# A layer of hybrid attention: transposed probabilities read back in one DMA instead of four

## The chip, the cores and the metric

One core of a Trainium2 chip runs the whole kernel. The metric is the device time of one execution in microseconds. The engines are named as in the profile: PE (TensorE; its weight loads are PEld), DVE (VectorE), ACT (ScalarE), POOL (GpSimd) and SP (SyncE, which here only issues DMAs).

## The reference, cut to what matters

One layer (DEPTH 1) works on x of 512 tokens by 1024 features, in float32:

```
h = rmsnorm(x); proj = h @ w_in              # columns go to groups A, B, C
A: 6 heads, dilated sliding-window attention, three (window, dilation) branches mixed by their denominators
B: 4 heads, gated linear attention in chunks
C: 6 heads, block attention: own block (causal) and the past blocks
x = x + concat(A, B, C) @ w_out
x = x + relu(rmsnorm(x) @ w_ff1)^2 @ w_ff2
return rmsnorm(x)
```

With 512 tokens the twelve heads of A and C can all be computed as causal attention over four query blocks and four key blocks of 128, with a bias table that counts how many branches see a distance. Each head needs, for every query block qb, scores against the keys up to its own block, an exponential P, and the product of P with the values. P comes out with queries on partitions; the product with the values needs keys on partitions. So P has to be transposed in blocks of 128 by 128.

## The kernel before, in words

Every matrix product in float32 precision is split into high and low parts and done as three faster products (names ending in h and l: wh and wl for weights, xh and xl, Ah and Al). The splitting keeps ACT and DVE busy all the time: ACT rounds (wh), DVE subtracts (wl).

The order of work comes from a planner written into the kernel. Generators ("streams") yield one operation at a time; the class Plan keeps a clock for each engine, gives each operation a cost (class Op), and issues the operation that can start first. So the order in each engine's queue is fixed when the program is built, from these modelled costs. `Shadow(op, sent)` plans with the cost of `op` but sends the operations in `sent` instead, or nothing when that is empty.

The stages are: the first projections and the norm (to 30 us), linear attention B (to about 105 us, partly beside the next one), the softmax attention of the twelve heads (about 87 to 190 us, with the query, key and value projections `qkps` and `vps` between), the output projection, and the feed-forward part in four steps to the end.

Heads are handled in pairs: p = 0 to 5, and e = 0, 1 within a pair. For each head, function `attention` computes the scores of query blocks 3, 2, 1, 0 on PE into two PSUM banks (tile `sps`, tag "s"), the widest first, 512, 384, 256 and 128 keys. Function `softmax` adds the bias and takes the row minimum on DVE in one instruction (the profile calls it CUSTOM_DVE_ANT_0, P<-sps,nb, followed by a short read of `mn`), which also frees the score bank, and then ACT forms the exponential in place.

The first five pairs (XP) are transposed by function `moved`; the last pair by PE itself. In `moved`, DVE transposes 32 by 32 blocks: for each of the four partition groups of 32 queries and each 32 keys, queries and keys change places. The results go to tile t (`tb` in the profile, blocks of query rows 3, 2 and 0) and to t2 (`t2s`, query block 1 of both heads of the pair). Since a 32 by 32 block cannot leave its group of 32 partitions, the rest of the transpose is done by way of HBM: SP stores the tile to a DRAM tensor (`turn`), and function `back` reads it to `thb` and `th` in the other order, issued by POOL. Writing a for the group of 32 queries, k for which 32 of a key block's 128 keys, j for the key among these and c for the rest, partition a*32+j of t holds columns (k, c); `back` wants partition k*32+j to hold columns (a, c). One access pattern over partitions cannot step through k and j with two different steps, so `back` issues four DMAs, one for each k, with 32 partitions each.

Function `values` then multiplies on PE (`po`), pairs (0, 1), (2, 3) and (4, 5) together, first the blocks from `thb`, then those from `th`. `mix_out` scales the result on DVE into `h`, from which the output projection follows.

SP's queue holds the stores of `turn`, the tables `nb`, the denominators (`zt`, `rzb`) and the loads of weights, in the planner's order. POOL's queue at that time holds nothing but the reads of `turn`.

Of the kernel before, what the change touches and what calls it, by code (L numbers as in the profile page):

```python
# [124 lines left out]
PE, ACT, DVE, POOL, SP = (Engine(n) for n in ("tensor", "scalar", "vector", "gpsimd", "sync"))  # L125


class Plan:
# [18 lines left out]
    def fire(self, key, t=None):  # L147
        self.done[key] = self.now if t is None else t

    def give(self, res):  # L150
        self.free[res].append(self.now)
# [79 lines left out]
def hybrid_block_kernel(ctx: ExitStack, tc: tile.TileContext, x0_d, xT_d, x_d, w0_d, wv_d, wqk_d, w1_d, w2_d,  # L231
# [13 lines left out]
    def slot(name, dt=F32, shape=(128, 512)):  # L245
        return sp.tile(list(shape), dt, name=name, tag="slot", bufs=SLOTS)

    def big(name, dt=F32, shape=(128, 1024)):
        return wp.tile(list(shape), dt, name=name, tag="big", bufs=BIGS)
# [741 lines left out]
    def attention(e):  # L991
# [7 lines left out]
        for p in range(6):  # L999
# [34 lines left out]
            if p in XP:  # L1034
                spawn(moved(p, e, P), 1)
                continue
# [86 lines left out]
    def moved(p, e, P):  # L1123

        yield ("take", "big")
        t, th = big("tb"), st["th", p, e]
        if ("t2", p) not in st:
            st["t2", p], st["th2", p] = slot("t2s"), slot("th2")
        t2, th2 = st["t2", p], st["th2", p]
        tv, t2v = (x.rearrange("p (k b j) -> p k b j", k=4, j=32) for x in (t, t2))  # L1130
        for qb, dst in ((3, tv[:, :, :4]), (2, tv[:, :, 4:7]), (1, t2v[:, :, 2 * e:2 * e + 2]), (0, tv[:, :, 7:])):
            yield ("wait", (p, e, qb))
            yield DVE.transpose(dst, P[qb].rearrange("p (b k j) -> p k b j", k=4, j=32))
        both = ("turned", p) in plan.done
        fire(("turned", p))
        d = dr.tile([128, 1024], F32, name=f"turn{2 * p + e}")
        yield SP.dma_start(d, t)
        give("big")
        if both:
            d2 = dr.tile([128, 512], F32, name=f"turn{12 + p}")  # L1140
            yield SP.dma_start(d2, t2)
            fire(("sent", p))
        yield from back(th, d)
        if both:
            yield from back(th2, d2)
            fire(("thx", p))

    def back(dst, d):
        n = d.shape[1]
        for k in range(4):  # L1150
            yield POOL.dma_start(dst[k * 32:k * 32 + 32].rearrange("p (a c) -> p a c", a=4),
                                 bass.AP(tensor=d.tensor, offset=d.offset + k * (n // 4), ap=[[n, 32], [32 * n, 4], [1, n // 4]]))

    def turned(pt, n, off, kbs, key):
        if kbs == (2,):
# [965 lines left out]
```

## Time and profile before

| | |
|---|---|
| median of 3 runs | 552.42 us (551.62 to 552.6) |
| profiled execution, its own time | 551.57 us |
| its span, first to last instruction | 549.8 us |
| busy: PE, DVE, ACT, POOL | 542.1, 486.5, 367.3, 94.6 us |
| granted TensorE clock, mean | 0.998 |
| read from HBM, written to it | 99.97 MB, 8.71 MB |

The profile is of one execution. "Busy" is time with an instruction on the engine. Each group of instructions has its outputs and inputs by name, its shape, a count, total busy microseconds and the mean nanoseconds of one, then the idle time of the engine just before and what ended it. Nearly all instructions carry line 158, the helper that sends them, so groups are told apart by tile names. In the timeline, a bracket at the end of a row gives idle time before the instruction and the instruction that ended it.

### The profile page before, as it was taken

Reading aid. Unit: us, or ns where it says so; the run is one execution under the profiler, and the core shown is the slowest. Engines: PE = TensorE matmul, PEld = TensorE weight load, DVE = VectorE, ACT = ScalarE, POOL = GpSimd, SP = SyncE. Lnnn points to the kernel's source line nnn. Section 1 sums busy time; section 2 is a strip of 40 time slices with the busy share of each in tenths; the row PEclk is TensorE's granted clock in tenths of the full one; section 3 lists DMA queues with packets and bytes.
Section 4 is the critical chain, followed back from the end, with each engine's and each line's share of the span. In section 5 each row is a group of like instructions: output and inputs, shape, how many; then the busy total and the mean of one; then the engine's idle time right before and its main releaser. Section 6 shows DMA issues by size and latency. Waiting matters only on the chain.

```text
span 549.8 us, 9220 instructions
## 1 busy us (share of the span) xinstructions
PE 542.1 (99%) x3362; PEld 474.2 (86%) x3362; DVE 486.5 (88%) x820; ACT 367.3 (67%) x628; POOL 94.6 (17%) x148
## 2 busy tenths in 40 slices
PE   9999999999999999999999999999999999999995
PEld 8988888888888788899988999888999888998884
DVE  6879998999987899899999869899679899589985
ACT  7756465668576566987965458773387863489844
POOL 7100000432624010230111100111100111202030
PEclk9999999999999999999999999999999999999999
DMA  8940304799998999889859934869744789976504
GB/s 294 395 161 2 115 1 134 223 272 256 272 310 280 345 348 241 156 227 255 234 124 287 278 60 149 229 154 268 191 110 159 161 226 246 195 167 169 103 0 153
DMA packets 35677, 109.28 MB, mean 199 GB/s; under 512 B 5266, under 2 KB 5952, under 8 KB 35632
## 3 DMA queue, kind: packets, MB, share of 16 engines
q1 hardware_dynamic: 25104, 74.81, 38.8%
q0 software_dynamic: 10240, 33.35, 31.6%
q8 instruction: 26, 0.43, 0.3%
q10 hardware_dynamic: 288, 0.53, 0.3%
q14 instruction: 19, 0.16, 0.1%
HBM read 99.97 MB, written 8.71 MB: 198 GB/s over the span
## 4 chain that ended last, share of the span: by engine, by line
PE 98%; DVE 1%; ACT 0%; issue 0%; DVEq 0%; ACTq 0%
PE f2X L158 19%; PE f1V L158 17%; PE qkps L158 12%; PE f2W L158 10%; PE vps L158 8%; PE f1W L158 8%; PE f2Y L158 5%; PE f1X L158 4%; PE sps L158 3%; PE po L158 2%; PE av L158 2%; PE lp L158 1%; PE bk L158 1%; PE bq L158 1%; PE op L158 1%; PE warm L158 1%
## 5 line engine op out<-in xcount | busy, mean ns | idle before, releaser
L158 DVE TENSOR_TENSOR wl<-w2raw,wh 128x1024 fp32r<-128x1024 f32 x56 | 67.8, 1221 | 3.3 <-ACT wh L158 3.0
L158 DVE TENSOR_TENSOR wl<-w1raw,wh 128x1024 fp32r<-128x1024 f32 x46 | 55.5, 1222 | 16.2 <-ACT wh L158 16.2
L158 PE MATMUL f1V<-Uh,wh 128*128 128x512 f32 (+1 forms) x240 | 69.1, 353 | 0.0
L158 POOL DMA_DIRECT2D w2raw<-in_w x36 | 31.6, 992 | 205.3 <-DVE wl L158 139.7
L158 ACT ACTIVATE wh<-w1raw 128x1024 fp32r<-128x1024 f32 x49 | 50.7, 1052 | 23.0 <-DVE w1raw L158 20.4
L158 ACT ACTIVATE wh<-w2raw 128x1024 fp32r<-128x1024 f32 x56 | 57.9, 1050 | 11.7 <-issue 5.1
L158 PE MATMUL f2X<-wh,Ah 128*128 128x512 f32 (+1 forms) x160 | 62.4, 390 | 0.0
L158 PE MATMUL f2X<-wh,Al 128*128 128x512 f32 (+1 forms) x160 | 61.9, 387 | 0.0
L158 PE MATMUL f2X<-wl,Ah 128*128 128x512 f32 (+1 forms) x160 | 61.9, 387 | 0.0
L158 PE MATMUL f1V<-Uh,wl 128*128 128x256 f32 x192 | 54.3, 283 | 0.0
L158 PEld LDWEIGHTS f1V<-Uh,wh 128*128 128x128 f32 x240 | 42.0, 189 | 5.8
L158 ACT ACTIVATE h<-h 128x512 f32<-128x512 f32 x56 | 35.2, 628 | 13.3 <-DVE h L158 12.6
L158 PE MATMUL qkps<-xh,wh 128*128 128x512 f32 x96 | 38.1, 397 | 0.0
L158 PE MATMUL qkps<-xh,wl 128*128 128x512 f32 x96 | 37.6, 391 | 0.0
L158 PE MATMUL qkps<-xl,wh 128*128 128x512 f32 x96 | 37.5, 391 | 0.0
L158 ACT ACTIVATE P<-P,mn 128x512 f32<-128x512 f32 (+3 forms) x48 | 26.6, 556 | 15.7 <-DVE mn L158 15.5
L158 PEld LDWEIGHTS f1V<-Uh,wl 128*128 128x128 f32 x192 | 36.4, 189 | 0.0
L158 PEld LDWEIGHTS f2X<-wh,Ah 128*128 128x128 f32 x160 | 30.1, 188 | 7.2 <-issue 1.2
L158 PEld LDWEIGHTS f2X<-wl,Ah 128*128 128x128 f32 x160 | 30.1, 188 | 6.2
L158 PEld LDWEIGHTS f2X<-wh,Al 128*128 128x128 f32 x160 | 30.1, 188 | 5.9
L158 ACT ACTIVATE Ah<-s 128x512 fp32r<-128x512 f32 x40 | 24.0, 622 | 12.8 <-DVE s L158 12.3
L158 POOL DMA_DIRECT2D thb<-turn x40 | 21.8, 552 | 59.7 <-DMA turn<-tb 41.5
(312 smaller groups left out, 1595.0 us busy)
## 6 DMA issues: line engine op xcount, KB each, us to landing
w2raw<-in_w SPq DMA_DIRECT2D x42, 512.0 KB
w2raw<-in_w POOLq DMA_DIRECT2D x36, 512.0 KB, 7.6
w1raw<-in_w SPq DMA_DIRECT2D x33, 512.0 KB
wraw<-in_wqk SPq DMA_DIRECT2D x12, 512.0 KB
turn<-tb SPq DMA_DIRECT2D x10, 512.0 KB
thb<-turn POOLq DMA_DIRECT2D x40, 128.0 KB, 5.0
w1raw<-in_w POOLq DMA_DIRECT2D x9, 512.0 KB, 6.3
wraw<-in_wv SPq DMA_DIRECT2D x8, 512.0 KB
```

The source lines that it names most:

```text
L158: getattr(getattr(self.nc, op.eng), op.method)(*op.args, **op.kw)
```

## The change

```diff
@@ moved
         for qb, dst in ((3, tv[:, :, :4]), (2, tv[:, :, 4:7]), (1, t2v[:, :, 2 * e:2 * e + 2]), (0, tv[:, :, 7:])):
             yield ("wait", (p, e, qb))
-            yield DVE.transpose(dst, P[qb].rearrange("p (b k j) -> p k b j", k=4, j=32))
+            yield DVE.transpose(dst, P[qb].rearrange("p (b j k) -> p k b j", k=4, j=32))
@@ back
         n = d.shape[1]
+        whole = POOL.dma_start(dst.rearrange("p (a c) -> p a c", a=4),
+                               bass.AP(tensor=d.tensor, offset=d.offset, ap=[[n // 4, 128], [32 * n, 4], [1, n // 4]]))
         for k in range(4):
-            yield POOL.dma_start(dst[k * 32:k * 32 + 32].rearrange("p (a c) -> p a c", a=4),
-                                 bass.AP(tensor=d.tensor, offset=d.offset + k * (n // 4), ap=[[n, 32], [32 * n, 4], [1, n // 4]]))
+            part = POOL.dma_start(dst[k * 32:k * 32 + 32].rearrange("p (a c) -> p a c", a=4),
+                                  bass.AP(tensor=d.tensor, offset=d.offset + k * (n // 4), ap=[[n, 32], [32 * n, 4], [1, n // 4]]))
+            yield Shadow(part, () if k else (whole,))
```

A key of a block was numbered k*32+j: block k held 32 neighbouring keys. Now it is j*4+k: block k holds every fourth key, starting at k. After the 32 by 32 transposes, key j*4+k stands on partition a*32+j in columns (k, c), that is, in DRAM at (a*32+j)*n + k*n/4 + c. With the partition q = j*4+k this is 32*a*n + q*n/4 + c: one step, n/4, over all 128 partitions. So one DMA reads what four did, to the same places as before, and the product with the values is unchanged.

DVE's transposes read P with the 32 elements of a block 16 bytes apart instead of 4; what they write has the same shape and place. There are 40 of them. The reads go from 60 DMAs to 15, of the same bytes and the same runs of 1 KB (512 bytes for the second tensor). The planner still sees four DMAs at their old costs, in `part`, and sends `whole` in place of the first.

## The prediction

> **What bounds the kernel now.** I read the page's head and chain first, then the list of who waited for whom on the matrix engine, then busy time by stretches.
>
> ```profile
> span 549.8 us, 9220 instructions
> PE 542.1 (99%) x3362; PEld 474.2 (86%) x3362; DVE 486.5 (88%) x820; ACT 367.3 (67%) x628; POOL 94.6 (17%) x148
> PE 98%; DVE 1%; ACT 0%; issue 0%; DVEq 0%; ACTq 0%
> PE warm L158 <- DVE eps L158: 1.1, 1, 1.1
> 268.00:540.00 272.00, 272.00 (x1546) 239.45 (x1545) 238.15 (x314) 179.00 (x270) 35.52 (x40) 1.00 0.67 169
> ```
>
> PE is the chain for 98% of the span, and the only wait of its matmuls that the list names is 1.1 us at the very start. From 268 to 540 us it is busy in all 272.00 us: a microsecond that PE loses earlier is never made up. So a gain has to come out of waits that PE hardly has, while a loss needs only an engine that falls behind PE. The change touches DVE, SP's data, POOL and the DMA queues during the attention stage, so the second view is that stage (columns: stretch, length, then busy time of PE, PEld, DVE, ACT, POOL).
>
> ```profile
> 94.68:106.00 11.32, 11.32 (x68) 9.89 (x67) 11.07 (x36) 10.08 (x27) 3.46 (x7) 1.00 0.57 189
> 106.00:122.00 16.00, 16.00 (x79) 13.52 (x79) 15.52 (x35) 8.79 (x16) 6.31 (x12) 1.00 0.95 287
> 122.00:149.00 27.00, 27.00 (x193) 23.17 (x192) 26.27 (x76) 18.41 (x47) 12.09 (x23) 1.00 0.95 262
> 149.00:164.00 15.00, 15.00 (x72) 12.48 (x71) 12.76 (x36) 11.04 (x27) 4.34 (x8) 1.00 1.03 294
> sum 69.32, PE 69.32 PEld 59.06 DVE 65.62 ACT 48.31 POOL 26.20; mean PE 17.33 PEld 14.76 DVE 16.40 ACT 12.08 POOL 6.55
> ```
>
> Here DVE is full too: 65.62 of 69.32 us, 3.70 us idle. Two engines are at their limit at once, and the coupling between them is tight:
>
> ```profile
> 94.68 1.17 DVE L158 STREAM_TRANSPOSE tb<-P 128x512 f32<-128x512 f32 x2
> 95.77 0.40 DVE L158 STREAM_TRANSPOSE t2s<-P 128x256 f32<-128x256 f32 x1
> 96.10 0.65 DVE L158 CUSTOM_DVE_ANT_0 P<-sps,nb 128x512 f32<-128x512 f32 x1
> 96.82 0.19 PEld L158 LDWEIGHTS sps<-k,q 128*128 128x128 f32 x1 [0.23 <-DVE mn L158]
> ```
>
> Transposes stand in DVE's queue directly ahead of the score minimum (P<-sps), which empties one of two score banks; PE's next score weights are loaded only when it has done so, and here PE's loader already waits 0.23 us for it. What a transpose takes longer, this wait takes longer.
>
> **The change, part by part.** (1) The transposes. Four per head, ten heads (five pairs p of two), all inside this stage:
>
> ```profile
> L158 DVE STREAM_TRANSPOSE tb<-P x30: 266/552/707, 94.7 to 162.8; 128x512 f32<-128x512 f32 x10, 128x384 f32<-128x384 f32 x10, 128x128 f32<-128x128 f32 x10
> 94.68:163.10 68.42, 14.96 (x30) 1.00 0.91 260
> 94.68:163.10 68.42, 4.05 (x10) 1.00 0.91 260
> ```
>
> They are busy for 14.96 + 4.05 = 19.01 us. Their count, sizes and destinations stay. The order in which they read P changes: the 32 elements of a block were neighbours (4 bytes apart), now each stands 16 bytes after the last. No DVE row of this trace reads in steps of 16 bytes, so the price is bounded. Nearest rows:
>
> ```profile
> 43.47 0.74 DVE L158 TENSOR_TENSOR e<-b 128x256 f32<-128x256 f32 x2
> 56.85 0.76 DVE L158 TENSOR_TENSOR e<-b 128x256 f32<-128x256 f32 x2
> L158 DVE TENSOR_TENSOR wl<-wraw,wh 128x1024 fp32r<-128x1024 f32 x8 | 9.6, 1218 | 0.0
> L158 DVE TENSOR_TENSOR la<-la,ab 128x512 f32<-128x512 f32 x1 | 0.7, 684 | 0.0
> L158 DVE TENSOR_TENSOR rg<-rg,gw 128x256 f32<-128x256 f32 x4 | 1.7, 425 | 0.1
> L158 DVE TENSOR_SCALAR sg<-rg 128x256 f32<-128x256 f32 x4 | 1.1, 286 | 0.0
> ```
>
> The seven levels of the linear attention read b in ever finer steps; the last, level 1, takes every second element (8 bytes), and its pair costs 0.76 us against 0.74 for a coarser level. So 8 bytes are as good as free; lower bound zero (a gain would need a pace that contiguous reads do not have). The pace: 1218 - 684 = 534 ns for 512 more elements, 1.04 ns each, one step per element. The fastest DVE row, sg, needs (425 - 286)/256 = 0.54 ns less per element than rg: it takes two neighbours, 8 bytes, per step. Both rows fit a reader that covers 8 bytes per step: then elements 8 bytes apart cost nothing and elements 16 bytes apart cost two steps. That is my estimate: 1.04 ns more per element. One head has 512 + 384 + 256 + 128 = 1280 elements per partition, so 1280 x 1.04 = 1.33 us more, ten heads 13.3 us. The upper end is the whole instruction doubled, fixed part too: 19.0 us. I take 13.3 because the fixed part has no reading in it.
>
> [...]
>
> How much of 13.3 us reaches PE? DVE's own pauses swallow some. Those that wait for PE in this stretch:
>
> ```profile
> 121.87 0.69 DVE L158 CUSTOM_DVE_ANT_0 P<-sps,nb 128x512 f32<-128x512 f32 x1 [0.16 <-PE sps L158]
> 124.41 0.56 DVE L158 CUSTOM_DVE_ANT_0 P<-sps,nb 128x384 f32<-128x384 f32 x1 [0.15 <-PE sps L158]
> 131.06 0.69 DVE L158 TENSOR_TENSOR tk<-qkps,R 128x512 f32<-128x512 f32 x1 [0.17 <-PE qkps L158]
> 149.35 0.69 DVE L158 TENSOR_TENSOR tk<-qkps,R 128x512 f32<-128x512 f32 x1 [0.43 <-PE qkps L158]
> 152.52 0.69 DVE L158 CUSTOM_DVE_ANT_0 P<-sps,nb 128x512 f32<-128x512 f32 x1 [1.17 <-PE sps L158]
> 156.85 0.42 DVE L158 CUSTOM_DVE_ANT_0 P<-sps,nb 128x256 f32<-128x256 f32 x1 [0.63 <-PE sps L158]
> ```
>
> They add up to 0.16 + 0.15 + 0.17 + 0.43 + 1.17 + 0.63 = 2.7 us (3.7 us with every small gap of the stretches above). I take 2.7: 13.3 - 2.7 = 10.6 us of delay for PE. DVE's longer pauses after 166 us help DVE catch up, not PE. What is queued behind a late transpose: on DVE the next minima and the splitting of weights, both awaited by PE; on SP the store of the turned tile, and behind it the loads of the next weights, which slip by as much as PE itself does.
>
> (2) The reads back. Fifteen groups of four DMAs become fifteen DMAs of the same bytes, so 45 issues on POOL go.
>
> ```profile
> L158 POOL DMA_DIRECT2D thb<-turn x40 | 21.8, 552 | 59.7 <-DMA turn<-tb 41.5 <-PE ptp L158 14.8 <-PE qkps L158 2.1
> L158 POOL DMA_DIRECT2D th<-turn x20 | 10.9, 550 | 1.3 <-issue 0.8 <-DMA thb<-turn 0.4
> L158 POOL DMA_DIRECT2D w2raw<-in_w x36 | 31.6, 992 | 205.3 <-DVE wl L158 139.7 <-DMA w2raw<-in_w 41.0 <-PE f2X L158 15.3
> 123.50 2.19 POOL L158 DMA_DIRECT2D th<-turn x4 [0.16 <-issue]
> DMA to landing us min/median/max: 5.1/7.7/8.3
> 134.94 0.61 PE L158 MATMUL po<-th,v 128*64 128x128 f32 x8
> ```
>
> POOL spends 32.7 us on sixty; fifteen at between 0.55 (today's) and 2.2 us (four times the pieces) cost 8 to 33 us, so POOL gets between 24 us and nothing back. I take 0.99, the row of a 512 KB DMA: 15 us. None of it is on the path: POOL is 17% busy and mostly waits for the store to land. The tightest of these transfers is the second pair's last: its fourth issue begins near 125.1 us, lands at most 8.3 us later, 133.4, and PE reads it at 134.94. So the cover is 1.5 us. Without it the cost would be one to one; but one DMA issued at 123.5 instead of a fourth at 125.1 adds 1.6 us of cover. Cost and gain: 0.
>
> The planner is fed the costs of the old DMAs through Shadow, so every queue keeps its order, less the dropped issues.
>
> Sum: +10.6 (transposes) + 0 (reads) = +10.6 us on the profiled run's own 551.57 us (span 549.8 and 1.8 around it): 562.2 us. The median of the runs shown is 552.42, 0.85 above that run; runs lie within 0.2% of each other, and that is what I call no change.
>
> **The rivals.** (a) No change, because reading every fourth element costs DVE nothing: 551.6 us. For it: the finest step in the trace is free, and the transposes run at (707 - 266)/384 = 1.15 ns per element, slower than other DVE rows, so the read might have a little room. Against: no row shows 16 bytes. [...] (b) A step of 16 bytes costs only half a step more per element: 6.7 - 2.7 = 4.0 us, 555.6 us. (c) The whole instruction doubles: 19.0 - 2.7 = 16.3, 567.9 us. (d) Faster: the read back lands earlier and fewer DMAs crowd the queues, which are 95 to 103% busy from 106 to 164 us, so PE stops waiting. It decides only if PE waits there; all its listed waits are 1.1 us, at the start, so at most 551.57 - 1.1 = 550.5 us. [...] (e) The merged DMA is worse: with four times the pieces it lands over 3.1 us (1.5 + 1.6) later than the fourth did. Five microseconds more would delay PE by about 2: 553.5 us.
>
> **How the numbers follow.** My forecast 0.52; (a) 0.24; (b) 0.10; (c) 0.06; (d) 0.04; (e) 0.04. The time is that of the forecast, 562.2 us; its own range, with absorption of 1 to 4 us and the size of one step uncertain, is 558 to 565. The range for 8 in 10 must take in (a), and reaches to (c): 551.0 to 568.0. Slower: 0.52 + 0.10 + 0.06 + 0.04 = 0.72; within 0.2%: 0.24; faster: 0.04.
>
> **What would show it.** The transposes' rows: 128x512 at about 1.24 us and 128x128 at 0.40 mean the forecast, 0.71 and 0.27 rival (a). The stretch from the first to the last transpose should grow by about 10 us, with PE's loader waiting for mn there and the part after 190 us keeping its length. POOL's thb row should show 10 issues, th 5. The prediction is wrong if transposes slow but PE does not wait, or if PE waits for thb or th.

## The result and the profile after

| | before | after |
|---|---|---|
| median | 552.2 us (4 runs, 551.62 to 552.6) | 559.57 us (4 runs, 559.05 to 559.84) |
| ratio | | 1.0134, 95% interval 1.0122 to 1.0146 |
| profiled execution, its own time | 551.57 us | 559.84 us |
| its span | 549.8 us | 557.9 us |

The changed kernel is slower by 7.4 us (6.7 to 8.1). The forecast was 562.2 us, +10.6. Start with the page of the kernel after, the rows of busy time and the shares of the chain that ended last:

```profile
span 557.9 us, 9125 instructions
PE 546.4 (98%) x3362; PEld 474.4 (85%) x3362; DVE 495.7 (89%) x820; ACT 367.4 (66%) x628; POOL 72.5 (13%) x103
PE 86%; DVE 8%; issue 2%; DMA 2%; ACT 1%; SPq 0%; DVEq 0%; ACTq 0%
```

The chain was PE for 98% before; now DVE has 8% of it. (The 2% of DMA is one load of output weights, `woraw`, that the chain passes through at 162 us; no pause of DVE ends with it.) The number of DVE's instructions is unchanged (820), its busy time is 9.2 us longer than the 486.5 before. POOL has 45 instructions fewer and 22.1 us less to do. So the reads back shrank as the change says, and DVE pays for something. The groups of VectorE in the stretch of the transposes say what; the figures after the first bar are total busy us and the mean ns of one:

```profile
L158 DVE STREAM_TRANSPOSE tb<-P 128x512 f32<-128x512 f32 x10 | 10.9, 1094 | 0.0
L158 DVE STREAM_TRANSPOSE tb<-P 128x384 f32<-128x384 f32 x10 | 8.5, 848 | 0.0
L158 DVE STREAM_TRANSPOSE t2s<-P 128x256 f32<-128x256 f32 x10 | 6.0, 598 | 0.0
L158 DVE STREAM_TRANSPOSE tb<-P 128x128 f32<-128x128 f32 x10 | 3.7, 373 | 0.0
```

The same four groups of the kernel before:

```profile
L158 DVE STREAM_TRANSPOSE tb<-P 128x512 f32<-128x512 f32 x10 | 7.0, 702 | 0.0
L158 DVE STREAM_TRANSPOSE tb<-P 128x384 f32<-128x384 f32 x10 | 5.5, 553 | 0.0
L158 DVE STREAM_TRANSPOSE t2s<-P 128x256 f32<-128x256 f32 x10 | 4.0, 405 | 0.0
L158 DVE STREAM_TRANSPOSE tb<-P 128x128 f32<-128x128 f32 x10 | 2.8, 279 | 0.0
```

Read each set as a fixed part and a slope. Before: (702 - 279)/384 = 1.10 ns per element and 138 ns fixed. After: (1094 - 373)/384 = 1.88 ns and 133 ns. Only the slope moved, by 0.78 ns per element. All forty together keep DVE busy for 28.74 us where it was 19.01: +9.73 us, or 0.76 ns for each of the 12,800 elements.

How much of it reached PE? Two stretches of the kernel after, the first from the start of the first transpose to a point behind the last, the second of 359 us up to nearly the end; then the same two of the kernel before. Columns: start and end, length, then busy us (and instructions) of PE, PEld, DVE, ACT and POOL, granted clock, DMA share, GB/s:

```profile
95.64:172.00 76.36, 72.78 (x407) 58.74 (x406) 74.51 (x180) 48.19 (x117) 9.05 (x12) 1.00 0.76 249
190.00:549.00 359.00, 358.97 (x2157) 317.50 (x2153) 318.73 (x430) 245.17 (x374) 47.29 (x54) 1.00 0.73 191
```

```profile
94.68:163.90 69.22, 69.22 (x405) 58.96 (x405) 65.52 (x180) 48.22 (x117) 26.20 (x48) 1.00 0.91 262
182.00:541.00 359.00, 358.96 (x2157) 317.59 (x2152) 318.71 (x430) 244.96 (x374) 47.91 (x54) 1.00 0.74 193
```

With the same 180 instructions of DVE, the first stretch lasts 76.36 us instead of 69.22: +7.14. The second is the same work at the same pace, so the loss arises in the first alone. (The spans differ by 8.1 us because this run reaches its first transpose 0.96 us later; runs without the new read start it between 94.68 and 95.73 us too.) PE, busy without a gap before, now has 76.36 - 72.78 = 3.6 us of gaps; the other 3.6 us are recorded as busy, though the matmuls are the same: those just behind a wait have longer records (`sps<-k,q` of 384 keys 409 ns on average instead of 368). DVE is busy 8.99 us longer (less than the 9.73 of the transposes alone, since an instruction's record may overlap the next one's: a transpose that starts at 170.31 us and lasts 0.62 is followed by one at 170.83) and its pauses shrink from 3.70 us to 1.85. Since the stretch is DVE's busy time plus its pauses, that gives 8.99 - 1.85 = 7.14. The sum alone doesn't say that DVE is the cause; the waits of PE's weight loader name the link; us in total, times, longest. First the kernel after, then the kernel before:

```profile
PEld sps L158 <- DVE mn L158: 7.4, 12, 1.4
```

```profile
PEld sps L158 <- DVE mn L158: 0.5, 2, 0.2
```

That is 6.9 us more, nearly all of the 7.14. The matmuls' own waits in the kernel after, of which the kernel before has none in this stretch:

```profile
PE sps L158 <- DVE mn L158: 3.4, 7, 1.0
```

The score banks `sps` come free when DVE has taken the row minimum `mn`; the minima stand in DVE's queue behind the longer transposes. No wait for `thb` or `th` appears.

### The profile page after: what moved, and what is told of

Read it like the earlier page. It is cut to its first block, busy times and chain, and to the rows that moved or that the text cites. A ratio compares the mean times of both kernels' runs of the same rounds, so it can differ in the third digit from the quotient of the medians.

```text
span 557.9 us, 9125 instructions
## 1 busy us (share of the span) xinstructions
PE 546.4 (98%) x3362; PEld 474.4 (85%) x3362; DVE 495.7 (89%) x820; ACT 367.4 (66%) x628; POOL 72.5 (13%) x103
## 4 chain that ended last, share of the span: by engine, by line
PE 86%; DVE 8%; issue 2%; DMA 2%; ACT 1%; SPq 0%; DVEq 0%; ACTq 0%
PE f2X L158 19%; PE f1V L158 16%; PE f2W L158 10%; PE f1W L158 8%; PE vps L158 7%; PE qkps L158 6%; PE f2Y L158 5%; PE f1X L158 4%; DVE tb L158 2%; PE av L158 2%; DVE P L158 2%; PE po L158 2%; DMA woraw<-in_w 2%; PE lp L158 1%; PE bk L158 1%
## 5 line engine op out<-in xcount | busy, mean ns | idle before, releaser
L158 ACT ACTIVATE wh<-w2raw 128x1024 fp32r<-128x1024 f32 x56 | 57.8, 1050 | 11.1 <-issue 5.1
L158 ACT ACTIVATE P<-P,mn 128x512 f32<-128x512 f32 (+3 forms) x48 | 26.7, 556 | 19.9 <-DVE mn L158 19.5
L158 DVE TENSOR_TENSOR wl<-wraw,wh 128x1024 fp32r<-128x1024 f32 (+1 forms) x28 | 29.7, 1067 | 1.7 <-ACT wh L158 1.6
```

The costliest lines, as they stand in the source:

```text
L158: getattr(getattr(self.nc, op.eng), op.method)(*op.args, **op.kw)
```

## Experiments

Two questions: what in the read costs 0.76 ns per element, and is it that alone that moves the end?

**The read back alone, and the transposes alone.** e_near_one keeps the transposes of the kernel before and merges the DMAs; e_far_four does the reverse.

```diff
  e_near_one, against before (back)
+        whole = POOL.dma_start(dst..., ap=[[n // 4, 128], [32 * n, 4], [1, n // 4]])
...
+            yield Shadow(part, () if k else (whole,))
  e_far_four, against before (moved, back)
-            yield DVE.transpose(dst, P[qb].rearrange("p (b k j) -> p k b j", k=4, j=32))
+            yield DVE.transpose(dst, P[qb].rearrange("p (b j k) -> p k b j", k=4, j=32))
...
-   offset=d.offset + k * (n // 4), ap=[[n, 32], [32 * n, 4], [1, n // 4]]
+   offset=d.offset + k * 32 * (n // 4), ap=[[n // 4, 32], [32 * n, 4], [1, n // 4]]
```

> The other half alone: transposes as before, one DMA over all 128 partitions in place of four. The keys then reach the wrong partitions, so the first five pairs multiply probabilities with the wrong values; all sizes and the order of work are those of the kernel after. Theory: no change from before, 552.2 us within 0.2%, transposes at 0.70 us, POOL 22 us less busy. Rival, the merged DMA is what costs: 559 us. Second rival, the merged DMA helps and the transposes hide it: below 551 us.

> Half of the change alone: the transposes read every fourth key, but the tile is read back in four DMAs of 32 partitions each (each a quarter of the merged one), as many and as large as before. Theory: the loss is all in the transposes, so 559.6 us within 1 us, 7.4 us over before, DVE transposes of 128x512 at 1.09 us, PE's loader waiting some 7 us for mn. Rival, the merged DMA is what costs (it lands late, or frees POOL at a bad time): 552 us.

Measured: e_near_one 552.18 us, ratio 1.0003 (0.9994 to 1.0012); e_far_four 558.89 us, ratio 1.0129 (1.0115 to 1.0143), beside 552.0 for the kernel before. The whole loss lies in the transposes, and the merged DMA is worth nothing either way. The widest transposes in e_near_one and then in e_far_four, and the loader's wait in e_far_four, where as many DMAs run as before:

```profile
L158 DVE STREAM_TRANSPOSE tb<-P 128x512 f32<-128x512 f32 x10 | 7.0, 703 | 0.0
```

```profile
L158 DVE STREAM_TRANSPOSE tb<-P 128x512 f32<-128x512 f32 x10 | 11.0, 1098 | 0.0
```

```profile
PEld sps L158 <- DVE mn L158: 7.3, 12, 1.4
```

**A step of 8 bytes.** e_second_two takes every second key, so each transpose reads 8 bytes apart, and two DMAs of 64 partitions bring a tile back.

```diff
-            yield DVE.transpose(dst, P[qb].rearrange("p (b k j) -> p k b j", k=4, j=32))
...
+            yield Shadow(part, (DVE.transpose(dst.rearrange("p (k h) b j -> p k b h j", h=2),
+                                              P[qb].rearrange("p (b h j k) -> p k b h j", h=2, k=2, j=32)),))
...
+            half = POOL.dma_start(dst[h * 64:h * 64 + 64]..., ap=[[n // 2, 64], [32 * n, 4], [1, n // 4]])
+            yield Shadow(part, () if k % 2 else (half,))
```

> Blocks of every second key: the transposes read elements 8 bytes apart, and the tile is read back in two DMAs of 64 partitions. [...] Rival, the price grows with the distance: a third of the way from 4 to 16 bytes, transposes of 128x512 at 0.83 us, about 3.2 us more of DVE and 2 to 2.5 us more in all, 554.5 us.

Measured: 551.97 us, ratio 0.9998 (0.9989 to 1.0007). Its rows on VectorE are those of the kernel before to the nanosecond:

```profile
L158 DVE STREAM_TRANSPOSE tb<-P 128x512 f32<-128x512 f32 x10 | 7.0, 702 | 0.0
L158 DVE STREAM_TRANSPOSE tb<-P 128x128 f32<-128x128 f32 x10 | 2.8, 279 | 0.0
```

**The price of a step by itself.** m_steps is no layer at all: it repeats single operations on a tile in SBUF, reading with steps of 1 to 16 elements (4 to 64 bytes), six times each, for 512 and for 256 elements. `view` and `flat` take every s-th element; the kinds `tw`, `w` and `aw` write with a step instead.

```diff
+        for kind in ("t", "tw", "ts", "tt", "w", "a", "aw"):
+            for s in (1, 2, 3, 4, 5, 6, 8, 12, 16):
...
+                        if kind == "t":
+                            nc.vector.transpose(y.rearrange("p (b j) -> p b j", j=32), view(x, s, n))
+                        elif kind == "ts":
+                            nc.vector.tensor_scalar(y, flat(x, s, n), 2.0, None, op0=OP.mult)
+                        elif kind == "tt":
+                            nc.vector.tensor_tensor(y, o[:, :n], flat(x, s, n), op=OP.mult)
+                        elif kind == "a":
+                            nc.scalar.activation(y, flat(x, s, n), AF.Copy)
...
```

> This kernel leaves the whole layer out. It runs on one tile of float32 only transposes, tensor_scalar, tensor_tensor (DVE) and activations (ACT), six times each, that read every 1st, 2nd, 3rd, 4th, 5th, 6th, 8th, 12th and 16th element (4 to 64 bytes apart), or write every 2nd, 4th, 8th, and the transposes of the two kernels in their own shapes. Its own time means nothing; its rows count. In the kernel after, the transpose of 128x512 takes 1094 ns against 702 with neighbouring elements. [...] Theory B, the reader walks over memory at 8 bytes per step (what the prediction assumed): 16 bytes two steps, 32 bytes four, 64 bytes eight, so the price doubles with the distance: 32 bytes 1.8 us, 64 bytes over 3 us. Theory C, only the transpose pays and tensor_tensor stays at 0.69 us at every distance.

Mean ns of one instruction of 512 elements, by step of the read in bytes, from the groups of DVE and ACT:

| | 4 | 8 | 12 | 16 | 20 | 24 | 32 | 48 | 64 |
|---|---|---|---|---|---|---|---|---|---|
| DVE transpose | 673 | 668 | 817 | 1048 | 1050 | 1047 | 1062 | 1034 | 998 |
| DVE tensor_tensor | 678 | 674 | 851 | 1085 | 1103 | 1124 | 1149 | 1122 | 1100 |
| DVE tensor_scalar | 386 | 404 | 427 | 597 | 606 | 600 | 612 | 590 | 582 |
| ACT activation | 617 | 648 | 874 | 1124 | 1123 | 1108 | 1115 | 1074 | 1043 |

Some of these groups as they stand, three of the transpose and one each of two others:

```profile
L39 DVE STREAM_TRANSPOSE t_two_full<-src 128x512 f32<-128x512 f32 x6 | 4.0, 668 | 0.0
L39 DVE STREAM_TRANSPOSE t_four_full<-src 128x512 f32<-128x512 f32 x6 | 6.3, 1048 | 0.0
L39 DVE STREAM_TRANSPOSE t_sixteen_full<-src 128x512 f32<-128x512 f32 x6 | 6.0, 998 | 0.0
L43 DVE TENSOR_TENSOR tt_four_full<-other,src 128x512 f32<-128x512 f32 x6 | 6.5, 1085 | 0.0
L45 ACT ACTIVATE a_four_full<-src 128x512 f32<-128x512 f32 x6 | 6.7, 1124 | 0.0
```

All four readers have the same shape: at 8 bytes free or nearly so (at most 31 ns, on ACT), part of the price at 12, about all of it at 16, and from there to 64 bytes the price stays within a fifth. At 12 bytes the price is 0.38 of that at 16 on the transpose, 0.43 on tensor_tensor, 0.51 on ACT and 0.19 on tensor_scalar. A rule by distance alone, every step over 8 bytes paying in full, doesn't fit the 12-byte column. A reader of 8 bytes per step doesn't fit either: its price would grow from 16 to 64 bytes or be a whole step of 1.04 ns, as the prediction estimated. And it is no property of the transpose. At 16 bytes an element costs (1048 - 673)/512 = 0.73 ns more on the transpose, 0.79 on tensor_tensor, 0.99 on ACT and 0.41 on tensor_scalar, whose 512 elements take 386 ns with neighbours where the others take over 600. The runs show the price by step; what in the reading of the memory sets it, they don't show.

m_steps also ran the transposes of 512 elements in the shapes of the kernels: reading neighbours (`near`), every second (`mid`) and every fourth element (`far`):

```profile
L61 DVE STREAM_TRANSPOSE near_d<-src 128x512 f32<-128x512 f32 x6 | 4.7, 783 | 0.0
L61 DVE STREAM_TRANSPOSE mid_d<-src 128x512 f32<-128x512 f32 x6 | 4.5, 757 | 0.0
L61 DVE STREAM_TRANSPOSE far_d<-src 128x512 f32<-128x512 f32 x6 | 7.0, 1167 | 0.0
```

Here the step of 16 bytes costs (1167 - 783)/512 = 0.75 ns per element, against (1094 - 702)/512 = 0.77 in the kernels.

**The same single DMA without the price.** Steps of 8 bytes cost the transpose nothing (668 ns against 673 in m_steps, 702 against 702 in e_second_two), and the step of 16 bytes can be made in two steps of 8. In e_split the operation that writes P reads the even keys first and then the odd ones, and the transposes read every second element of that.

```diff
  against the changed kernel (softmax, moved)
-        yield DVE.tensor_tensor_reduce(P, s, nb, 1.0, 3e38, OP.add, OP.min, mn)
...
+        a, b = "p (m k) -> p k m", "p (k m) -> p k m"
+        even = DVE.tensor_tensor_reduce(P.rearrange(b, k=2), s.rearrange(a, k=2), nb.rearrange(a, k=2), ..., mn)
+        yield Shadow(part, (even if key[0] in XP else part,))
...
-            yield DVE.transpose(dst, P[qb].rearrange("p (b j k) -> p k b j", k=4, j=32))
...
+            half = DVE.transpose(dst.rearrange("p (h k) b j -> p k h b j", h=2),
+                                 P[qb].rearrange("p (k b j h) -> p k h b j", h=2, k=2, j=32))
+            yield Shadow(part, (half,))
```

> The changed kernel (one DMA back per tile, blocks of every fourth key), but the step of 16 bytes is split in two steps of 8: the operation that writes P (sum of scores and bias, with its minimum) takes the even keys of both inputs first, then the odd ones, and writes them side by side; the transposes then read every second element of P. The order of the queues is that of the changed kernel. [...] Rival 1 (the price hangs on the distance from key to key, wherever it is paid): the minima take over some of it, 40 operations at up to 0.39 us more, 555 to 560. Rival 2 (scores are read from PSUM, where no run here shows a step; an 8-byte step may cost there): the minima alone grow, by up to 0.5 ns per element, 12,800 elements in all, 6 us, of which some 4 reach TensorE: 556.

Measured: 552.21 us, ratio 1.0002 (0.9993 to 1.0011). Transposes and minima in the stretch, and the DMAs on POOL:

```profile
L158 DVE STREAM_TRANSPOSE tb<-P 128x512 f32<-128x512 f32 x10 | 7.0, 702 | 0.0
L158 DVE CUSTOM_DVE_ANT_1 P<-sps,nb 128x512 f32<-128x512 f32 x8 | 5.3, 684 | 1.3 <-PE sps L158 1.3
...
L158 POOL DMA_DIRECT2D thb<-turn x10 | 7.6, 757 | 73.2 <-DMA turn<-tb 64.3 <-PE yp L158 7.8 <-DMA turn<-t2s 1.0
```

The transposes are at 702 ns, the minima at 684 where the kernel before has 680, with one DMA per tile. So the price hangs on how far apart successive accesses are, not on the distance from key to key; and an 8-byte step from PSUM costs next to nothing either (the 4 ns). The kernel is level with the one before, since the merged DMA had nothing to give.

**From DVE's time to PE's.** Three runs vary how much DVE work is added, and where. The first two make the transposes of two pairs alone read every fourth element (`back` still issues four DMAs, over the matching rows); the third sends each transpose of the kernel before twice.

```diff
  e_two_first: far = p < 2;  e_two_last: far = p > 2
+            far = ...
+            yield DVE.transpose(dst, P[qb].rearrange("p (b j k) -> p k b j" if far else "p (b k j) -> p k b j", k=4, j=32))
...
  e_twice
+            part, again = (DVE.transpose(...) for _ in range(2))
+            yield Shadow(part, (part, again))
```

> The kernel before, with the transposes of the pairs p = 0 and 1 alone (four of the ten heads) reading every fourth element; all reads back are four DMAs, as before. Extra work on VectorE: 4 heads x 0.97 us = 3.9 us. Theory: a pause of VectorE swallows delay only if it lies behind the far transposes and TensorE is not late itself by then. In the changed kernel the pauses that remained lie at the last pair (0.61 and 0.63 us), and those that went are the ones in between. So with only the first pairs late, little is swallowed: delay 3.0 to 3.6 us, 555.0 to 555.6 against 552.0. Rival 1, a fixed toll: any pause of the stretch swallows, 1.85 us of them as in the changed kernel, so 2.0 us, 554.0. Rival 2: TensorE's loader has slack of its own, and less than 4 us never reaches it: 552.0.

> The kernel before, with the transposes of the pairs p = 3 and 4 alone (four of the ten heads) reading every fourth element; reads back as before. Extra work on VectorE: again 3.9 us. Theory (pauses swallow by place): the pauses of 0.43, 1.17 and 0.63 us that VectorE has in the kernel before lie in this part, behind some of these transposes, and one of them swallows what came before it: delay 1.5 to 2.8 us, 553.5 to 554.8, less than with the first two pairs. Rival 1 (fixed toll): 2.0 us, 554.0, the same as with the first two pairs. Rival 2 (proportional, 7.6 of 9.7 us reach TensorE wherever they arise): 3.0 us, 555.0, for both.

> The kernel before, with each of the forty transposes of probabilities issued twice in a row, reading neighbours as before; nothing else. It tests whether VectorE's time in this stretch goes to TensorE whatever makes it longer. Extra work on VectorE: the 19.0 us of the transposes once more. Theory (one to one, less the pauses): 19.0 - 1.85 to 2.7 = 16.3 to 17.2 us, so 568 to 569 against 552. Rival 2 (proportional, 7.6 of 9.7): 15 us, 567. Rival 3, the delay of the changed kernel comes from a property of the strided read itself (a port held, other engines slowed) rather than from VectorE being busy: then the extra time of plain transposes could hide, at most 5 us, 557.

Measured, beside 552.37 for the kernel before: e_two_first 554.83 us, ratio 1.0046 (1.0034 to 1.0059), +2.5; e_two_last 554.92, ratio 1.0043 (1.0030 to 1.0056), +2.5; e_twice 571.83, ratio 1.0358 (1.0344 to 1.0372), +19.5. The two small ones cost the same within their intervals (1.9 to 3.3 and 1.7 to 3.1 us), so the times alone rule out only that nothing arrives; both lie just outside the forecasts, 555.0 to 555.6 and 553.5 to 554.8. The stretch from the first transpose on, one row each of e_two_first, e_two_last and e_twice, tells more:

```profile
94.87:167.00 72.13, 70.15 (x405) 58.75 (x405) 69.09 (x180) 48.18 (x117) 26.18 (x48) 1.00 0.87 254
```

```profile
95.50:167.20 71.70, 70.79 (x407) 58.92 (x406) 69.15 (x180) 48.20 (x117) 26.21 (x48) 1.00 0.89 263
```

```profile
95.00:185.40 90.40, 80.45 (x407) 65.05 (x406) 85.59 (x222) 48.60 (x118) 26.17 (x48) 0.91 0.74 215
```

| | DVE's work more | DVE's pauses, us | stretch longer |
|---|---|---|---|
| e_two_first | 3.57 | 3.70 to 3.04 | 2.91 |
| e_two_last | 3.63 | 3.70 to 2.55 | 2.48 |
| the changed kernel | 8.99 | 3.70 to 1.85 | 7.14 |
| e_twice | 19.85 | 3.70 to 4.81 | 20.96 |

(The row of e_twice runs 0.22 us further than the others, over two more instructions; the table leaves that out.) The first three fit the theory that a pause swallows by its place: 0.66 us goes with the first pairs, 1.15 with the last, together 1.81 of the 1.85 of the whole change. In e_two_first the short pauses up to 125 us go (0.14, 0.11, 0.16 and 0.15 us); in e_two_last these stay, and the one of 0.43 us goes. A toll of 1.85 us each does not fit; a share of 7.14/8.99 of the work (2.8 and 2.9 us) fits the first and misses the second by 0.4, in one profile of each. The late pause at which they part, in e_two_first and then in e_two_last, was 1.17 us before:

```profile
155.64 0.69 DVE L158 CUSTOM_DVE_ANT_0 P<-sps,nb 128x512 f32<-128x512 f32 x1 [1.17 <-PE sps L158]
```

```profile
153.97 0.69 DVE L158 CUSTOM_DVE_ANT_0 P<-sps,nb 128x512 f32<-128x512 f32 x1 [0.63 <-PE sps L158]
```

With the first pairs late it stays whole, because PE, its releaser, is late by as much; with the last pairs late, 0.54 us of it goes.

e_twice settles that a property of the strided read beyond its length is not needed: plain transposes do the same harm, 19.5 us of time for 19.85 us of work. It missed my figure, 568 to 569. The pauses did swallow: of those over 0.1 us, 3.07 us in all before, 0.62 is left. But three things came on top of the forecast: the work was 19.85 us where I had counted 19.0; small pauses of DVE, most of them at the doubled transposes, add 1.45 us; and one new pause of 2.11 us. So the pauses grew by 2.11 + 1.45 - 2.45 = 1.11 us. One of the four groups of transposes, its idle time last (0.0 in the kernel before):

```profile
L158 DVE STREAM_TRANSPOSE tb<-P 128x512 f32<-128x512 f32 x20 | 14.1, 706 | 0.3
```

Two stretches and the new pause:

```profile
94.00:106.00 12.00, 8.75 (x42) 6.56 (x40) 11.56 (x34) 8.07 (x22) 2.22 (x4) 1.00 0.28 96
106.00:118.00 12.00, 11.83 (x50) 11.02 (x50) 9.76 (x28) 3.62 (x11) 5.62 (x11) 0.57 0.84 261
```

```profile
117.08 0.42 DVE L158 CUSTOM_DVE_ANT_0 P<-sps,nb 128x256 f32<-128x256 f32 x1 [2.11 <-PE sps L158]
```

PE waits for more than 3 of the first 12 us; in the next 12 the granted clock is 0.57, and VectorE, the late engine until then, has to wait 2.11 us for scores. So in this execution a lower clock came on top of PE's pauses. It took 573.1 us, 1.3 above the median; the other three were granted 0.994 over the whole run against 0.983 here. In the changed kernel the clock was 1.00 throughout the stretch.

**A plan that knows the price.** e_told gives the planner the transposes' true duration.

```diff
+            if method == "transpose" and n > 32:
+                self.cost = 0.06 + n * 1.88 / 1000
```

> The changed kernel, with the planner told the true duration of its transposes (0.06 us + 1.88 ns per element and partition, where the kernel has 0.075 us + 1.04 ns); so the order of all queues is planned anew. Theory: in this stretch TensorE has under 4 us of pauses in 77 and VectorE under 2, so no order can bring back much: 557 to 560 us. Rival: the delay is one of order (minima behind transposes that could have gone later), and a plan that knows the price hides most of it: 553 to 555 us.

Measured: 574.44 us, ratio 1.0399 (1.0383 to 1.0415). Both expectations fall: the new order is 15 us worse than the old one, with as many instructions on each engine. Two stretches of e_told:

```profile
94.50:145.00 50.50, 50.50 (x312) 43.43 (x312) 48.59 (x109) 32.68 (x76) 4.55 (x6) 1.00 0.59 188
145.00:190.00 45.00, 32.94 (x126) 25.40 (x125) 32.49 (x93) 22.28 (x62) 6.74 (x9) 0.70 0.86 277
```

To 145 us nothing is lost; in the 45 us behind it PE stands still for 12 us and DVE for 12.5, and the clock falls to 0.70. Two things happen there, one after the other. Up to 167.8 us DVE is busy for 21.77 of 22.80 us, and PE stands still for 6.1 us, in each pause waiting for DVE (the longest, 2.12 us, for `mn`): DVE is the late engine, as in the changed kernel, only more so. Then DVE itself stands still for 5.6 us, for the transfer of the denominators, and PE for 5.4 us, for `q`, which stands in DVE's queue behind that wait:

```profile
173.44 0.21 DVE L160 STREAM_TRANSPOSE rzt<-rz 128x32 f32<-128x32 f32 x1 [5.60 <-DMA zt<-rzt]
```

This shows one worse order; whether a better one exists it doesn't show. Which cost in the planner misled it wasn't tried, and stays open.

## Why the prediction was right in kind and high in size

- The step named as the cause held: transposes slower in proportion to their elements with the fixed part unchanged (138 and 133 ns), PE's loader waiting for `mn`, the time behind the stretch unchanged, no wait for `thb` or `th`. The 128x512 row was named as 1.24 us for the forecast and 0.71 for rival (a); it came out at 1.094. The measured 559.57 us lies in the forecast's own range, 558 to 565.
- The term that was mis-sized is the price per element: 1.04 ns forecast, 0.76 measured, so 9.7 us instead of 13.3. The inference was at fault: from the rows of `rg` and `sg` the prediction took a reader that covers 8 bytes per step, so that an element 16 bytes from the last costs a whole step more. That was the author's estimate, and m_steps contradicts it: on the transpose the price is 0.73 ns at 16 bytes, below a step, and doesn't grow to 64 bytes, where it is 0.63. The rows agreed with "8 bytes are free" (0.76 against 0.74 us); none of them held a price for 16. Rival (b), half a step or 0.52 ns, missed the size by 0.24 ns to the other side, where the forecast missed it by 0.28.
- The pauses: 2.7 us forecast as swallowed, 1.85 measured. The prediction counted the six pauses it listed as wholes; of their 2.7 us, 1.5 went, and the rest of the 1.85 came from shorter ones that it had left out. Those of 1.17 and 0.63 us late in the stretch became 0.61 and 0.63, because by then PE came late too (the same two instructions, in the kernel after):

```profile
158.73 0.69 DVE L158 CUSTOM_DVE_ANT_0 P<-sps,nb 128x512 f32<-128x512 f32 x1 [0.61 <-PE sps L158]
163.07 0.42 DVE L158 CUSTOM_DVE_ANT_0 P<-sps,nb 128x256 f32<-128x256 f32 x1 [0.63 <-PE sps L158]
```

- A third term was missing: instructions overlap at their ends, so 9.73 us of transposes keep DVE busy only 8.99 us longer.
- From 10.6 us forecast to 7.1 measured: -3.6 for the price (13.3 to 9.7), -0.7 for the overlap, +0.85 for the pauses. The last two nearly cancel, which is luck; the price carries the miss. The medians give 7.4.
- The reads back at zero: confirmed by e_near_one. Fifteen issues of about 0.75 us take 11.3 us of POOL, where 15 had been taken from the row of another 512 KB DMA; that made no difference. The rivals fall: (a) by the transposes' rows, (d) and (e) by e_near_one, (c) since the fixed part stayed, (b) by the price per element, 0.76 and not 0.52 ns.

## What to carry to other kernels

When an access pattern is changed to suit a DMA, price the reading side too: in these runs a float32 read with steps of 16 to 64 bytes cost DVE's transpose 0.63 to 0.76 ns, its tensor_tensor 0.79 to 0.92, its tensor_scalar 0.38 to 0.44 and ACT 0.83 to 0.99 ns more per element and partition, while steps of 8 bytes were free or nearly so (at most 31 ns in 512 elements), and a step of 16 could be made of two free ones (e_split, 702 ns). Fewer DMAs brought nothing where no engine waited for them (e_near_one, 552.18 us against 552.0). On an engine 95% busy that feeds the bounding one, most of the added work came out at the end: 2.5 of 3.6 us, 7.1 of 9.0, 19.5 of 19.9; and a pause swallowed delay only where its releaser was not late as well.

## What the hardware showed that I had not expected

- The price hardly changes from 16 to 64 bytes (+375 ns and +325 on the transpose of 512 elements), and is partial at 12 (+144).
- The writing side of the transpose pays like the reading side. Transposes in m_steps that write with a step of 8 bytes, and then of 16, in its timeline:

```profile
80.93 0.70 DVE L49 STREAM_TRANSPOSE dst<-src 128x512 f32<-128x512 f32 x1
...
89.99 1.05 DVE L49 STREAM_TRANSPOSE dst<-src 128x512 f32<-128x512 f32 x1
```

- The issue of a DMA on POOL grows with its pieces, but slowly: 550 ns for 32 partitions (before), 622 for 64 (e_second_two), 757 for 128 (e_split), about 2.1 ns per partition, with four pieces each.
- Short pauses of PE went before a lower granted clock. Two waits of the weight loader in e_twice, and the clock (third figure from the end) in a stretch just behind:

```profile
98.98 0.19 PEld L158 LDWEIGHTS sps<-k,q 128*128 128x128 f32 x1 [2.06 <-DVE mn L158]
105.60 0.19 PEld L158 LDWEIGHTS sps<-k,q 128*128 128x128 f32 x1 [2.03 <-DVE mn L158]
```

```profile
107.30:117.70 10.40, 10.40 (x45) 9.72 (x45) 8.15 (x25) 2.31 (x6) 5.32 (x10) 0.52 0.82 262
```

The gaps of PE at these two waits were 1.64 and 1.61 us. Later in e_twice the clock was 0.90 from 140 to 155 us, where PE stood still for 2.51 us, and 0.90 from 170 to 186 us, with 2.26 us; from 128 to 140 us, with 0.79 us, it was 1.00. In the pages of before, after, e_far_four, e_near_one, e_second_two, e_two_first, e_two_last, e_twice and e_told, the clock has a slice below 0.9 ahead of the last one only in e_twice and e_told. Their longest waits of a matmul in this part were 1.9 us (e_twice, for `mn`) and 5.4 us (e_told, for `q`); the longest in the changed kernel, 0.97 us, was followed by no fall (1.00 from 121 to 127 us and from 126 to 130). No run varies the waits alone, so whether they brought the lower clock is not shown.
